# Second channel-mix product by Strassen: seven half-width products per pair of tiles, weight sums on VectorE, and a new placement of the tiles in SBUF

## The chip, the core and the metric

The kernel runs on one NeuronCore of a Trainium2 chip. TensorE does the matrix products and accumulates into PSUM; VectorE (DVE), ScalarE (ACT) and GpSimd (POOL) do the elementwise work; SyncE (SP) and ACT issue the DMAs. Each engine works through its own queue in order and waits on semaphores for the others. The metric is the device time of one execution in microseconds. Before the change it is 2437.73 us, the median of three runs (2437.52 to 2438.23).

## The reference

512 tokens of width 1024 pass through two layers. All inputs, weights and results are float32.

```
for i in range(DEPTH):                       # DEPTH = 2
    h = rmsnorm(x, norm1_g[i]);  z = h @ w_in[i] + b_in[i]
    y_m = mLSTM branch (4 heads, 256 wide)   # scores, decay, values, head norm, output gate
    y_r = retention branch (4 heads, 256 keys, 512 values)
    merged = sigmoid(gm) * (y_m @ w_bm[i]) + sigmoid(gr) * (y_r @ w_br[i])
    x = x + merged @ w_out[i]
    h2 = rmsnorm(x, norm2_g[i])
    x = x + square(relu(h2 @ w_ff1[i] + b_ff1[i])) @ w_ff2[i] + b_ff2[i]     # 1024 -> 4096 -> 1024
    h3 = rmsnorm(x, norm3_g[i])
    x = x + sigmoid(h3 @ w_pe_gate[i]) * (p[i] @ w_pe[i])
return rmsnorm(x, final_g)
```

The change is in the product with `w_ff2`, in the order of the retention gates, and in where tiles lie.

## The kernel before

Activations lie transposed, features on partitions and the 512 tokens on the free axis. A weight tile of 128 rows by 128 columns is the stationary operand and 512 tokens stream past it. For accuracy each float32 operand is kept as two float32r parts, `hi` (a rounded copy that ACT makes) and `lo` (the rest, `src - hi`, that DVE makes). A product is three matmuls, hi by hi, hi by lo and lo by hi (`mm3`, lines 195 to 198).

Weights come as a stream of units of 128 by 1024 floats, 512 KB each, in the order of use. `load_unit` (from line 166) issues the DMA of a unit on SP into one of four raw buffers (`wr`), then has ACT copy it to `wh` (line 183) and DVE subtract to get `wl` (line 185); there are three buffers of each. `unit` keeps two units ready beyond the one in use. `t8` multiplies the 8 activation tiles with one unit: 24 matmuls into one PSUM bank of 8.

The layer runs in program order on TensorE: the projections, the mLSTM heads, the retention heads, the merge (`br_tile`, with the eight sigmoid gates of the retention branch kept on chip in `sB`), the out projection (`wo`), the channel mix, the embedding. The tile framework writes the waits and may move an instruction of another engine ahead of one that is not ready; on the chip the queues then run in the order that it wrote.

The channel mix takes the 4096 hidden columns in four blocks of 1024. For a block, eight `t8` calls make the hidden tiles (`l0f`, `l1f`): DVE multiplies the PSUM tile with the reciprocal root (line 745), ACT adds the bias and takes the relu (746), POOL squares (747), and `split` (210, 211) makes hi and lo. Then eight more `t8` calls multiply the hidden tiles with a unit of `w_ff2` each (`l0fo`, `l1fo`), and DVE adds each result into the residual `x` (777 for the first block, 779 for the others). In the last block each finished tile of `x` goes at once to the operands and squares of the third norm (`Norm.tile`, lines 241, 242, 254, 260). Then come the two `PE` units (the product with `p`), the third norm's `finish` and `spread`, and the gate product `pg`. At the very end four units of weights stay on chip and are used twice, with 256 tokens each time (`pl`).

In SBUF all pools exist for the whole kernel. The value tiles `vh`, `vl` and the temporaries are 516 floats wide, and `mh`, `ml` (the operand of `wo`) use the slots of the query and key tiles for four tiles and those of the value tiles for the other four.

Of the kernel before, what the change touches and what calls it, by code (L numbers as in the profile page):

```python
# [22 lines left out]
P = 128  # L23
# [6 lines left out]
EPS = 1e-6  # L30
UN = 1024
LOOK = 2
LAST = 4

# columns of w_in
# [3 lines left out]
# columns of the per-partition vectors  # L39
# [9 lines left out]

def unit_list():  # L50
    """What each unit of the weight stream holds, in the order of use (one layer)."""
# [48 lines left out]
    full("w_in", CGR)  # L100
# [11 lines left out]
    full("w_br", 0, 1024)  # L112
    full("w_out")
    for b in range(4):
        full("w_ff1", b * 1024)
        full("w_ff2", 0, b * 1024)
    u.append(("PE", 0))
    u.append(("PE", 1))
    full("w_pe_gate")
# [3 lines left out]
def build(ctx, tc, ins, out):  # L123
    nc = tc.nc
    ve, ac, gp, te = nc.vector, nc.scalar, nc.gpsimd, nc.tensor
    units = unit_list()
# [4 lines left out]

    cpool = pool("const", 1)
    wpool = pool("w", 3)
    apool = pool("act", 8)
    bpool = pool("big", 2)
    spool = pool("head", 4)
    tpool = pool("tmp", 7)
    opool = pool("one", 1)
    cols = pool("cols", 2)
    psum = pool("ps", 8, space=bass.MemoryType.PSUM)  # L140

    xs_dram = tc.dram_tile([KT, P, T], F32, name="x_spill")

# [10 lines left out]
    sel = cpool.tile([H, H, P], F32R, name="sel")  # L154
    cos = cpool.tile([P, T], F32, name="cos")
    sin = cpool.tile([P, T], F32, name="sin")
# [4 lines left out]
    def tmp(name, shape=(P, 516)):  # L161
        return tpool.tile(list(shape), F32, name=name, tag="t")

# [1 line left out]
    ready = []  # L165
    nxt = [0]

    def load_unit():
        n = nxt[0]
        if n >= L * NU:  # L170
            return
        nxt[0] += 1
        raw = wpool.tile([P, UN], F32, name=f"wr{n}", tag="wr", bufs=4)
        nc.sync.dma_start(raw, ins["wstream"][n])
        if n >= L * NU - LAST:
            hi = [apool.tile([P, T], F32R, name=f"wh{n}{a}", tag="Ah") for a in range(2)]
            lo = [apool.tile([P, T], F32R, name=f"wl{n}{a}", tag="Al") for a in range(2)]
            for a in range(2):
                split(raw[:, a * T:(a + 1) * T], hi[a], lo[a])
            ready.append((units[n % NU], hi, lo))  # L180
            return
        wh = wpool.tile([P, UN], F32R, name=f"wh{n}", tag="wh")
        ac.activation(wh, raw, AF.Copy)  # L183
        wl = wpool.tile([P, UN], F32R, name=f"wl{n}", tag="wl")
        ve.tensor_sub(wl, raw, wh.bitcast(F32))  # L185
        ready.append((units[n % NU], wh, wl))

    def unit(kind):
        while len(ready) < LOOK + 1 and nxt[0] < L * NU:
            load_unit()  # L190
        u, wh, wl = ready.pop(0)
        assert u[0] == kind, (u, kind)
        return u, wh, wl
# [15 lines left out]
    def split(src, hi_ap, lo_ap):  # L209
        ac.activation(hi_ap, src, AF.Copy)  # L210
        ve.tensor_sub(lo_ap, src, hi_ap.bitcast(F32))

    def acts(side, name):
        hi, lo = [], []
        for k in range(KT):
            hi.append(apool.tile([P, T], F32R, name=f"{name}h{k}", tag=f"{side}h"))
            lo.append(apool.tile([P, T], F32R, name=f"{name}l{k}", tag=f"{side}l"))
        return hi, lo

# [1 line left out]
    class Norm:  # L221
        """Of the token tiles j0 .. j1 - 1."""

        def __init__(self, name, side, i, gain, j0=0, j1=NT):
# [3 lines left out]
            self.act = acts(side, name) if side else None  # L228
# [15 lines left out]
        def square(self, k, x, pool=False):  # L244
            w = self.n * P
            x = x[:, self.s]
            if self.sum is None:
                sq = opool.tile([P, T], F32, name=f"{self.name}sum", tag="bv" if self.s.start else "ssum")[:, :w]
# [26 lines left out]
        def spread(self):  # L275
            n = self.name
            w = self.n * P
            dh = opool.tile([P, 1280], F32R, name=f"{n}dh", tag="ph")[:, :w]
# [198 lines left out]
    for i in range(L):  # L477
# [214 lines left out]
        for c in range(KT):  # L692
            gate_tile(sB, c, "bgr")
# [255 lines left out]
```

## Time and profile before

| | before |
|---|---|
| median of three runs | 2437.73 us |
| profiled execution, first to last instruction | 2435.6 us |
| TensorE matmul busy | 2412.0 us (99%), 11068 records |
| DVE busy | 1349.9 us (55%) |
| ACT busy | 928.9 us (38%) |
| POOL busy | 231.0 us (9%) |
| HBM read | 226.30 MB, 95 GB/s over the span |

The profiled execution gives its span, from its first to its last instruction; the three runs are timed from outside, 2.1 us longer in the median. Matmuls are pipelined: the profile shows each as 0.39 us long for 512 columns, but the next one starts sooner, so the time of a stage is read from start to start or from a window, never from the mean duration. DVE and ACT instructions also start a little before the end of the one ahead of them. In the rows, PE is TensorE's matmuls, PEld its weight loads, and "idle before" is the time in which the engine did nothing just ahead of the instruction, with what ended it.

### The profile page before, as it was taken

How to read it: one execution, taken by the hardware profiler on the slowest of the kernel's cores; microseconds unless marked ns; L12 is line 12 of the kernel's file. 1: busy time of each engine (PE TensorE's matmuls, PEld its weight loads, DVE VectorE, ACT ScalarE, POOL GpSimd, SP SyncE). 2: the span in 40 equal slices, each digit the busy share in tenths (PEclk: the TensorE clock that was granted, in tenths of full speed). 3: DMA queues.
4: the chain of work that ended last, by engine and by line, in shares of the span. 5: the costliest groups of instructions: out<-in, count | busy, mean ns of one | idle time of the engine just before them, and what ended most of it. 6: DMA issues, size and time to landing. Idle time of an engine off the chain costs nothing.

```text
span 2435.6 us, 27773 instructions
## 1 busy us (share of the span) xinstructions
PE 2412.0 (99%) x11068; PEld 2006.5 (82%) x11068; DVE 1349.9 (55%) x1974; ACT 928.9 (38%) x1280; POOL 231.0 (9%) x277
## 2 busy tenths in 40 slices
PE   8999999999999999999999999999999999999997
PEld 6888888888888888888888888888888888888887
DVE  7867534666455434435578665446665554434445
ACT  3756323333233423324547552223323333223343
POOL 4000000000000201102101000000000011101122
PEclk9999999999999999999999999999999999999999
DMA  4222232322223333333322222322322242333331
GB/s 165 91 89 77 87 102 89 95 82 90 92 79 123 102 98 100 97 95 104 126 82 91 89 82 93 101 87 87 96 87 87 81 134 89 100 99 95 95 105 52
DMA packets 69498, 232.30 MB, mean 95 GB/s; under 512 B 7540, under 2 KB 9972, under 8 KB 69368
## 3 DMA queue, kind: packets, MB, share of 16 engines
q1 hardware_dynamic: 64040, 220.95, 29.1%
q10 hardware_dynamic: 5328, 9.57, 1.2%
q8 instruction: 87, 1.43, 0.2%
q14 instruction: 43, 0.35, 0.0%
HBM read 226.30 MB, written 4.19 MB: 95 GB/s over the span
## 4 chain that ended last, share of the span: by engine, by line
PE 98%; DVE 1%; ACT 0%; DVEq 0%; POOL 0%; issue 0%; ACTq 0%
PE l1f L196 2%; PE l1f L198 2%; PE l0f L198 2%; PE l1fo L198 2%; PE l0fo L198 2%; PE l0f L196 2%; PE l0fo L197 2%; PE l0f L197 2%; PE l1fo L197 2%; PE l1fo L196 2%; PE l1f L197 2%; PE l0fo L196 2%; PE l0br L196 1%; PE l1br L196 1%; PE l1br L197 1%; PE l0br L197 1%
## 5 line engine op out<-in xcount | busy, mean ns | idle before, releaser
L183 ACT ACTIVATE wh<-wr 128x1024 fp32r<-128x1024 f32 x402 | 426.4, 1061 | 1105.5 <-issue 210.2
L185 DVE TENSOR_TENSOR wl<-wr,wh 128x1024 fp32r<-128x1024 f32 x402 | 493.3, 1227 | 174.6 <-ACT wh L183 172.6
L196 PE MATMUL l1f<-l1n2h,wh 128*128 128x512 f32 x256 | 99.7, 389 | 0.0
L196 PE MATMUL l0f<-l0n2h,wh 128*128 128x512 f32 x256 | 99.7, 389 | 0.0
L198 PE MATMUL l0f<-l0n2h,wl 128*128 128x512 f32 x256 | 99.6, 389 | 0.0
L198 PE MATMUL l1f<-l1n2h,wl 128*128 128x512 f32 x256 | 99.6, 389 | 0.0
L197 PE MATMUL l0f<-l0n2l,wh 128*128 128x512 f32 x256 | 99.6, 389 | 0.0
L197 PE MATMUL l1f<-l1n2l,wh 128*128 128x512 f32 x256 | 99.6, 389 | 0.0
L747 POOL TENSOR_TENSOR l1ft<-l1ft 128x512 f32<-128x512 f32 x32 | 45.8, 1431 | 255.9 <-ACT l1ft L746 251.8
L747 POOL TENSOR_TENSOR l0ft<-l0ft 128x512 f32<-128x512 f32 x32 | 45.7, 1431 | 255.9 <-ACT l0ft L746 251.8
L197 PEld LDWEIGHTS l0f<-l0n2l,wh 128*128 128x128 f32 x256 | 48.1, 188 | 10.1
L197 PEld LDWEIGHTS l1f<-l1n2l,wh 128*128 128x128 f32 x256 | 48.1, 188 | 10.1
L198 PEld LDWEIGHTS l1f<-l1n2h,wl 128*128 128x128 f32 x256 | 48.1, 188 | 10.0
L198 PEld LDWEIGHTS l0f<-l0n2h,wl 128*128 128x128 f32 x256 | 48.0, 188 | 10.0
L196 PEld LDWEIGHTS l0f<-l0n2h,wh 128*128 128x128 f32 x256 | 48.1, 188 | 9.9
L196 PEld LDWEIGHTS l1f<-l1n2h,wh 128*128 128x128 f32 x256 | 48.1, 188 | 9.9
L779 DVE TENSOR_TENSOR l1x<-l1fo,l1x 128x512 f32<-128x512 f32 x24 | 16.6, 691 | 67.1 <-PE l1fo L198 67.1
L779 DVE TENSOR_TENSOR l0x<-l0fo,l0x 128x512 f32<-128x512 f32 x24 | 16.6, 691 | 66.0 <-PE l0fo L198 66.0
L745 DVE TENSOR_TENSOR l0ft<-l0f,l0n2rb 128x512 f32<-128x512 f32 x32 | 22.0, 691 | 35.7 <-PE l0f L198 35.7
L745 DVE TENSOR_TENSOR l1ft<-l1f,l1n2rb 128x512 f32<-128x512 f32 x32 | 22.0, 691 | 35.6 <-PE l1f L198 35.6
L711 DVE TENSOR_TENSOR l0brt<-l0br,l0sB 128x512 f32<-128x512 f32 x16 | 11.1, 692 | 36.2 <-PE l0br L198 36.2
L711 DVE TENSOR_TENSOR l1brt<-l1br,l1sB 128x512 f32<-128x512 f32 x16 | 11.1, 691 | 36.2 <-PE l1br L198 36.2
(2001 smaller groups left out, 6852.7 us busy)
## 6 DMA issues: line engine op xcount, KB each, us to landing
wr<-wstream SPq DMA_DIRECT2D x406, 512.0 KB, 3.5
x<-xT SPq DMA_DIRECT2D x4, 512.0 KB, 5.9
l0xr<-xT ACTq DMA_DIRECT2D x8, 256.0 KB, 2.5
x_spill<-l0x ACTq DMA_DIRECT2D x8, 256.0 KB, 2.8
l1xr<-x_spill ACTq DMA_DIRECT2D x8, 256.0 KB, 2.6
out<-l1x SPq DMA_DIRECT2D x4, 256.0 KB, 2.6
out<-l1x SPq DMA_DIRECT2D x2, 384.0 KB, 3.9
l0pt<-pT ACTq DMA_DIRECT2D x2, 256.0 KB, 2.7
```

The lines of the kernel that those rows point to most:

```text
L183: ac.activation(wh, raw, AF.Copy)
L185: ve.tensor_sub(wl, raw, wh.bitcast(F32))
L196: te.matmul(o, sh, mh, start=first, stop=False)
L197: te.matmul(o, sh, ml, start=False, stop=False)
L198: te.matmul(o, sl, mh, start=False, stop=last)
L711: ve.tensor_tensor(t[:, :T], o, sB[:, c, :], OP.mult)
L745: ve.tensor_tensor(t[:, :T], o, n2.b, OP.mult)
L747: gp.tensor_tensor(t[:, :T], t[:, :T], t[:, :T], OP.mult)
L779: ve.tensor_tensor(x[:, c, :], o, x[:, c, :], OP.add)
```

## The change

**The second product of the channel mix.** Two output tiles of 128 columns form a pair, and for a block of 1024 hidden rows the pair's product is done by a Strassen scheme (in Winograd's form): the weights are split in four quarters (even or odd hidden tile, first or second output tile), the tokens in two halves of 256, and seven products of half size take the place of eight. One product is 4 tiles times 3 matmuls, 12 matmuls of 256 tokens.

- Weights: a pair takes two units of the stream (the same bytes as before). From them come four pieces: `B11` (a quarter, 512 wide) and `t1`, `t2`, `t3` (1024 wide each, two sums or quarters side by side). DVE makes four sums of 512 columns; each piece is then split into hi (ACT) and lo (DVE).
- Hidden tiles: two neighbouring tiles give eight quarters of 256 columns, four plain and four sums (`pair_operand`); seven of them, hi and lo, are kept.
- Results: the seven products run in three PSUM banks, and four of them (P3, P4, P6, P7) are added on top of what a bank already holds. DVE adds the bank into a 256-token half of `x` after every product: seven adds of 256 columns, and a product that accumulates on a bank must wait until the add before it has read it.
- Order: `pair_schedule` puts P4 of a pair behind P1 of the next one. The first hidden pair of the next block is computed ahead of the four output pairs of a block, and ahead of the last block's output pairs come the two `PE` units.

**The first product** makes two hidden tiles at a time; relu and square are both on ACT, and POOL does neither.

**The retention gates** are computed in the merge loop instead of being kept in `sB`; the first half of the product with `w_br` is written to DRAM and read back, eight tiles of 256 KB each way and layer.

**Placement.** Value tiles are 576 floats wide instead of 516, a 64-byte `pad` comes ahead of the weight buffers, and a tile of 16 or 48 floats (`shift`) moves the tiles of the channel mix. Pools are opened and closed by phases of the layer, on alternate sides of SBUF, with temporaries in the pool of the phase (two of them in the channel mix); `sel`, `cos` and `sin` are loaded once per layer.

**The weight stream** is prepared by pieces (`prep_next`, `ready`); two units instead of one are loaded ahead of `x` at the start.

```diff
+PRODUCTS = {"P1": ("B11", 0, 0), "P2": ("t1", 1, 2), "P3": ("t2", 1, 6), "P4": ("t3", 1, 1), "P5": ("t1", 0, 4),
+            "P6": ("t2", 0, 5), "P7": ("t3", 0, 3)}
+PIECE = ("B11", "t1", "t2", "t3")
+READY = {"P1": 2, "P4": 0, "P5": 3, "P2": 3, "P6": 5, "P3": 5, "P7": 6}
+def pair_schedule(n):
+    out = []
+    for i in range(n):
+        out.append((i, "P1"))
+        if i:
+            out.append((i - 1, "P4"))
+        out += [(i, x) for x in ("P5", "P2", "P6", "P3", "P7")]
+    out.append((n - 1, "P4"))
+    return out
...
+    def prep_next():
...
+        if x in PIECE:
+            r1, r2 = raws[n, 0], raws[n, 1]
+            c0, c1 = slice(0, Q), slice(Q, UN)
+            if x == "B11":
+                src, out_ = r2[:, c0], piece(cur["xw"], "b", Q)
+            elif x == "t1":
+                raws[n, "t"] = t = cur["xw"].tile([P, UN], F32, name=f"t{n}", tag="t")
+                ve.tensor_tensor(t[:, c0], r1[:, c0], r2[:, c1], OP.add)
+                ve.tensor_tensor(r1[:, c0], r1[:, c0], r2[:, c0], OP.add)
+                src, out_ = r1, piece(wpool, "w")
+            elif x == "t2":
+                ve.tensor_tensor(r2[:, c0], r1[:, c0], r2[:, c1], OP.add)
+                src, out_ = r2, piece(wpool, "w")
+            else:
+                src, out_ = raws.pop((n, "t")), piece(cur["xw"], "t")
+                ve.tensor_tensor(src[:, c1], r2[:, c0], r1[:, c1], OP.add)
...
+        split(src, *out_)
...
+        def product(self, x):
+            w, half, j = PRODUCTS[x]
+            ready(place[self.n, "B11"] + READY[x])
+            wh, wl = [a[:, half * Q:(half + 1) * Q] for a in pieces[self.n, w]]
+            b = {"P2": "b", "P5": "c", "P3": "c"}.get(x, "a")
+            first = x in ("P1", "P2", "P5")
+            if first:
+                self.bank[b] = ps(f"{self.name}{b}")
+            o = self.bank[b][:, 0:S]
+            m = slice(j * S, (j + 1) * S)
+            for k in range(4):
...
+                te.matmul(o, wh[:, s], h[:, m], start=f, stop=False, skip_group_check=True)
+                te.matmul(o, wh[:, s], l[:, m], start=False, stop=False, skip_group_check=True)
+                te.matmul(o, wl[:, s], h[:, m], start=False, stop=e, skip_group_check=True)
+            self.done(x, o)
...
+    def pair_operand(name, st, hi, lo):
+        v = st.rearrange("p (q t) -> p q t", t=S)
+        ve.tensor_tensor(v[:, 4:6, :], v[:, 1:3, :], v[:, 0:1, :].to_broadcast([P, 2, S]), OP.subtract)
+        ve.scalar_tensor_tensor(v[:, 6, :], v[:, 5, :], -1.0, v[:, 1, :], OP.mult, OP.subtract)
+        ve.scalar_tensor_tensor(v[:, 7, :], v[:, 6, :], -1.0, v[:, 3, :], OP.mult, OP.subtract)
+        split(st[:, 4 * S:8 * S], hi[:, 3 * S:7 * S], lo[:, 3 * S:7 * S])
+    def pair_quarters(st, hi, lo):
+        split(st[:, S:4 * S], hi[:, 0:3 * S], lo[:, 0:3 * S])
...
-        vh = [spool.tile([P, 516], F32R, name=f"{nm}vh{j}", tag="vh") for j in range(NT)]
+        vh = [cur["low"].tile([P, 576], F32R, name=f"{nm}vh{j}", tag="vh", bufs=NT) for j in range(NT)]
...
-    load_unit()
+    fill_raws(2)
     for k in range(0, KT, 2):
         nc.sync.dma_start(x[:, k:k + 2, :], ins["xT"][k:k + 2].rearrange("k p t -> p k t"))
...
+            o = t8(yr, f"l{i}br0{c}")
+            ac.activation(t[:, :T], o, AF.Copy)
+            nc.scalar.dma_start(br_dram[i, c], t[:, :T])
...
-            br_tile(c, yr)
+            nc.scalar.dma_start(t[:, :T], br_dram[i, c])
+            g = gated(f"l{i}gr{c}", t8(xa, f"l{i}gr{c}"), n1, AF.Sigmoid, bcol(i, "bgr", c))
+            o = t8(yr, f"l{i}br1{c}")
+            ve.tensor_tensor(t[:, :T], o, t[:, :T], OP.add)
+            ve.tensor_tensor(t[:, :T], t[:, :T], g[:, :T], OP.mult)
+            ve.tensor_tensor(mA[:, c, :], mA[:, c, :], t[:, :T], OP.add)
...
-            gp.tensor_tensor(t[:, :T], t[:, :T], t[:, :T], OP.mult)
-            split(t[:, :T], hid[0][c], hid[1][c])
+                ve.tensor_tensor(a, o, n2.b, OP.mult)
+                ac.activation(a, a, AF.Relu, bias=bcol(i, "bf1", 8 * b + 2 * p + d))
+                ac.activation(a, a, AF.Square)
...
+                def done(x_, o):
+                    if x_ in ("P1", "P2"):
+                        add(1, o, OP.add)
+                    elif x_ == "P5":
+                        add(2, o, OP.subtract)
+                    elif x_ in ("P6", "P3"):
+                        add(3, o, OP.subtract)
+                    elif x_ == "P7":
+                        add(2, o, OP.subtract)
+                    elif x_ == "P4":
+                        add(0, o, OP.add)
+                        if b == 3:
+                            for c in (2 * p, 2 * p + 1):
+                                n3.tile(c, x[:, c, :])
```

More of the change, by code (lines that the diff above doesn't have):

```diff
@@ L30 @@
 EPS = 1e-6
+Q = 512
+S = 256
 UN = 1024
 LOOK = 2
+RAWS = 4
+PIECES = 3
+PAD = 16
 LAST = 4
@@ L188, in unit, with tmp, split @@
-    def unit(kind):
-        while len(ready) < LOOK + 1 and nxt[0] < L * NU:
-            load_unit()
-        u, wh, wl = ready.pop(0)
-        assert u[0] == kind, (u, kind)
-        return u, wh, wl
+    def tmp(name, dt=F32):
+        return cur["tmp"].tile([P, T], dt, name=name, tag="t", bufs=cur["ntmp"])
+    def split(src, hi_ap, lo_ap):
+        ac.activation(hi_ap, src, AF.Copy)
+        ve.tensor_sub(lo_ap, src, hi_ap.bitcast(F32))
+    order, loads = [], []
+    for n, u in enumerate(units):
+        if u[0] == "PAIR":
+            order += [(n, x) for x in PIECE]
+            loads += [(n, 0), (n, 1)]
+        else:
+            order.append((n, 0))
+            loads.append((n, 0))
@@ L195, in mm3, with ready @@
+    def ready(k):
+        while at["prep"] < min(len(order), k + 1):
+            prep_next()
+    def unit(kind):
+        n = at["unit"]
+        at["unit"] += 1
+        assert units[n][0] == kind, (units[n], kind)
+        ready(place[n, 0] + LOOK)
+        return units[n], *pieces.pop((n, 0))
     def mm3(o, sh, sl, mh, ml, first, last):
@@ L247, in square @@
             if self.sum is None:
-                sq = opool.tile([P, T], F32, name=f"{self.name}sum", tag="bv" if self.s.start else "ssum")[:, :w]
+                sq = opool.tile([P, T], F32, name=f"{self.name}sum", tag="ssum" + self.half)[:, :w]
             else:
@@ new lines, in ff2, with make, add @@
+        def ff2(b, p):
+            def make(n):
+                nm = f"l{i}o{b}{p}"
+                started = set()
+                def add(q, o, op):
+                    y = x[:, 2 * p + q // 2, (q % 2) * S:(q % 2 + 1) * S]
+                    if b == 0 and q not in started:
+                        started.add(q)
+                        ve.scalar_tensor_tensor(y, y, bcol(i, "bf2", 2 * p + q // 2), o, OP.add, op)
+                    else:
+                        ve.tensor_tensor(y, y, o, op)
+                def done(x_, o):
[12 more added lines that the diff above has]
+                                n3.tile(c, x[:, c, :])
+                return Pair(nm, n, [hid[b, k] for k in range(4)], done)
+            return make
```

357 lines of the change are left out of this document (213 added, 144 removed).

## The prediction

> **What bounds the kernel now.** I read the page's head first, then the shares of the chain of work that ended last, then windows over the stages that the change touches, then single rows of the timeline.
>
> ```profile
> span 2435.6 us, 27773 instructions
> ...
> PE 2412.0 (99%) x11068; PEld 2006.5 (82%) x11068; DVE 1349.9 (55%) x1974; ACT 928.9 (38%) x1280; POOL 231.0 (9%) x277
> ...
> DVE  7867534666455434435578665446665554434445
> ...
> PEclk9999999999999999999999999999999999999999
> ...
> PE 98%; DVE 1%; ACT 0%; DVEq 0%; POOL 0%; issue 0%; ACTq 0%
> ```
>
> TensorE is busy for 99% and 98% of the last chain is matmuls, at full granted clock in every slice. Nothing else can shorten this kernel: a gain has to come out of TensorE's own time. DVE is half idle on average, in the channel mix (slices 14 to 19 and 34 to 39) 30 to 50% busy.
>
> The next rows are windows (window; its length; busy us and instructions of PE, PEld, DVE, ACT and POOL; clock, DMA share, GB/s): the first output stage of the channel mix, the out projection, the whole channel mix of layer 0. Below them, two rows of the timeline (start, duration): the first of 84 matmuls of 256 columns at the kernel's end, and the one that follows the 84th.
>
> ```profile
> 854.80:898.30 43.50, 43.50 (x193) 36.04 (x192) 16.45 (x17) 9.74 (x11) 1.47 (x1) 1.00 0.29 97
> ...
> 764.70:808.90 44.20, 44.20 (x193) 36.04 (x192) 21.19 (x25) 17.06 (x23) 11.38 (x15) 1.00 0.46 144
> ...
> 808.90:1159.40 350.50, 350.50 (x1555) 290.45 (x1554) 154.69 (x179) 118.55 (x147) 56.97 (x42) 1.00 0.31 98
> ```
> ```profile
> 2395.37 0.28 PE L196 MATMUL pl<-l1n3h,wh 128*128 128x256 f32 x1
> ...
> 2405.45 0.28 PE L196 MATMUL pl<-l1n3h,wh 128*128 128x256 f32 x1
> ```
>
> 192 matmuls of 512 tokens take 43.50 us, 0.2266 us each, with no gap; 84 of 256 tokens take 10.08 us, 0.120 us each, with a weight load for each. So a half-width matmul costs 0.53 of a full one: seven half-size products for eight do not save an eighth.
>
> **The change, part by part.** (1) *Matmuls of the second product.* Removed: 2 layers x 4 blocks x 192 matmuls, 8 x 43.50 = 348.0 us. Added: 2 x 16 pairs x 84 matmuls, 32 x 10.08 = 322.6 us. TensorE's floor falls by **25.4 us**. [...]
>
> (2) *Alignment.* In the out projection half of the 192 matmuls read operands from 516-float slots: 44.20 us against 43.50, 0.70 us a layer.
>
> ```profile
> 690.50:697.60 7.10, 7.08 (x30) 5.55 (x30) 1.78 (x3) 1.00 0.26 75
> ```
>
> This is a retention head's product with the values, also from 516-float slots: 30 matmuls in 7.10 us where 30 x 0.2266 is 6.80. Eight heads and two projections give up to 8 x 0.30 + 2 x 0.70 = 3.8 us; some of a head's 0.30 is a wait at its end, so I take **-2.5 us**. The new kernel also shifts the channel mix's operands by 16 or 48 floats. Were that as bad as the 516-float slots (0.70/96 = 7.3 ns a matmul), 2688 matmuls would lose 19.6 us; I take 0, since all the new widths are multiples of 64 floats, like the tiles that run at 0.2266.
>
> (3) *DVE in a pair.* Spacing of DVE instructions from start to start, then durations by group and the 256-column add:
>
> ```profile
> 1504.34 0.68 DVE L599 TENSOR_TENSOR l1r0brku<-l1r0brku,l1r0brkw 128x512 f32<-128x512 f32 x1
> 1504.95 0.74 DVE L598 SCALAR_TENSOR_TENSOR l1r0brkw<-l1r0brkz,bc,cos 128x512 f32<-128x512 f32 x1
> 1505.61 1.21 DVE L185 TENSOR_TENSOR wl<-wr,wh 128x1024 fp32r<-128x1024 f32 x1
> 1506.75 0.68 DVE L211 TENSOR_TENSOR l1r0kl<-l1r0brku,l1r0kh 128x512 fp32r<-128x512 f32 x1
> ```
> ```profile
> L185 DVE TENSOR_TENSOR wl<-wr,wh 128x1024 fp32r<-128x1024 f32 x402 | 493.3, 1227 | 174.6 <-ACT wh L183 172.6
> ...
> L802 DVE TENSOR_TENSOR l1pgt<-pl,l1n3rb 128x256 f32<-128x256 f32 x8 | 3.4, 422 | 4.1 <-PE pl L198 3.9
> ```
>
> In a stream a 512-column operation costs DVE 0.61 us, a 1024-column one 1.14, and a 256-column add some 0.34 (0.42 less the same 0.08 of overlap). A pair needs four sums (2.44), four lo parts (0.61 + 3 x 1.14 = 4.03) and seven adds (2.38): **8.85 us of DVE in 10.08 us of TensorE**, 88%. Two tiles before took 2 x 1.14 + 2 x 0.61 = 3.5 us in 10.9. In the last block two norm operands come on top (2 x 0.66): 10.2 us, over the limit by a little. The hidden pairs need 2 x 0.61 for the root, 0.87 + 1.14 for lo, 0.61 + 2 x 0.40 for the sums and 2 x 1.14 for the weights, 6.9 us in 10.9. So DVE fits, in the output stage barely; what decides is whether it is free at the moments that TensorE needs it.
>
> (4) *The accumulating banks.* P7 lands on the bank that P6 filled, with P3 between them; P4 on the bank of P7, with the next pair's P1 between. How fast the add is done shows at the end of the 256-token products and at the start of the kernel:
>
> ```profile
> 2406.76 0.28 PE L198 MATMUL pl<-l1n3h,wl 128*128 128x256 f32 x1
> 2406.89 0.28 PE L196 MATMUL pl<-l1n3h,wh 128*128 128x256 f32 x1
> ...
> 2407.16 0.42 DVE L802 TENSOR_TENSOR l1pgt<-pl,l1n3rb 128x256 f32<-128x256 f32 x1 [1.16 <-PE pl L198]
> ```
> ```profile
> 11.65 8.05 DVE L242 SCALAR_TENSOR_TENSOR l0n1l<-x,bc,l0n1h 128x512 fp32r<-128x512 f32 x5
> ...
> 19.76 0.50 PE L197 MATMUL l0if<-l0n1l,wh 128*128 128x512 f32 x1 [0.72 <-DVE l0n1l L242]
> ```
>
> The free DVE starts 0.27 us after the next product's slot began (2407.16 - 2406.89), takes 0.42, and TensorE follows 0.06 later (19.76 after 19.70): 0.75 us. A product between them lasts 12 x 0.12 = 1.44, so 0.69 us of slack. In the last pair of a group P4 follows P7 with nothing between: 0.75 us of idle, 4 groups a layer, **+6.0 us** in all; this one nothing can hide. For the other 24 P4 and 32 P7 the bounds are 0 (DVE free) and 0.54 each (the add waits behind a full lo part, 1.23 + 0.75 - 1.44), 0 to 30 us. DVE is inside one of its three long lo parts for a third of the time, and only the first 0.54 us of such a part is harmful: I take 0.1 us each, **+5.6 us**.
>
> (5) *Pieces of weights.* A sum on DVE, the hi copy on ACT and the lo part on DVE are a chain for t1, t2 and t3. `B11` and `t3` have one buffer each, t1 and t2 share three. `t3` can be started when P4 of the pair before has ended (1.44 us of slots after P1) and is needed by P7: 2.88 to 8.64 on the pair's clock, for a chain of about 1.06 + 1.23 + 0.1. t1 of the next pair follows it (sums 1.22, 1.06, 1.23) and is needed at 12.96. Both fit with 3 us to spare if DVE fills ACT's time with other work. In the group's first pair the lo parts of the hidden tiles compete. **+4 us** for the entries of 8 groups and for the third norm's last two tiles (below), between 0 and 13 us: 8 x 1.23 + 2 x 1.6.
>
> (6) *ACT and POOL.* POOL's squares go to ACT:
>
> ```profile
> L183 ACT ACTIVATE wh<-wr 128x1024 fp32r<-128x1024 f32 x402 | 426.4, 1061 | 1105.5 <-issue 210.2
> ...
> L747 POOL TENSOR_TENSOR l0ft<-l0ft 128x512 f32<-128x512 f32 x32 | 45.7, 1431 | 255.9 <-ACT l0ft L746 251.8
> ...
> L241 ACT ACTIVATE l0n3h<-l0x,bc 128x512 fp32r<-128x512 f32 x8 | 5.7, 709 | 0.0
> ```
>
> An output pair gives ACT 3 x 1.06 + 0.63 = 3.8 us of 10.08, a hidden pair under 7 of 10.9: no bound, 0. POOL loses its longest link (1.43 us per tile).
>
> (7) *Moved work.* The two `PE` units go ahead of the last four pairs, with the same 48 matmuls. They covered the third norm's end: now the gate product starts right behind the last P4 and needs tile 6 after 18 x 0.2266 = 4.1 us, for an add, ACT 0.71 and DVE 0.74, some 2.2 us with waits. Covered unless DVE is over 1.6 us behind; that is in (5). The gates of the retention branch move to the merge loop: same matmuls; eight 256 KB writes and reads a layer on ACT's queue; the chain of the last tile grows to three DVE steps, ACT and a lo part, 3 x 0.69 + 0.63 + 0.68, under the 7 x 0.68 = 4.8 us before the out projection needs it: 0. At the layer boundary SP waits for the old pool's tiles before it loads `sel`, with the weight units behind it; four raw buffers and the prepared pieces hold over 20 us of TensorE's work: 0. At the start a second unit of 512 KB goes ahead of `x` (GB/s in 40 slices of the first 25 us):
>
> ```profile
> GB/s 0 0 5 153 111 386 402 397 393 400 410 410 383 390 393 403 413 413 413 341 371 377 413 400 406 413 321 0 0 0 0 0 0 0 0 197 341 282 98 164
> ```
>
> 512 KB at 400 GB/s is 1.3 us, part of it in the slow first slices of the queue: **+1.0 us**, between 0 and 2.
>
> **Sum.** -25.4 - 2.5 + 6.0 + 5.6 + 4.0 + 1.0 = -11.3 us against the profiled 2435.6: 2424.3. The runs' median lies 2.1 us above that span, so **2426 us**, 0.5% faster.
>
> **The rivals.** *All waits but the bare one vanish* (adds always find DVE free, entries and start cost nothing): -25.4 - 2.5 + 6.0, 2416 us. For it: 12% of DVE is free in a pair, and the written order can put the adds first. Against: each lo part is 1.23 us that cannot be interrupted.
>
> *The gain is eaten at the group ends*: each of the 8 last P4 waits for a full lo part of the next stage's weights too, 8 x 1.98 = 15.8 instead of 6.0: 2436 us, no change. For it: just then the queue prepares three units. Against: it would have to hit all eight.
>
> *DVE becomes the bound.* Its waits for ACT between a sum and a lo part stay uncovered: each is 1.06 + 0.14 = 1.2 us, and in the row of line 185 DVE does wait for ACT, 172.6 us over 402 parts. With one of three uncovered a pair takes 8.85 + 1.2 = 10.05, still under 10.08; with two 11.25, 32 x 1.17 = 37.4 us in place of the 5.6: 2458 us; with three 12.45 and 2497 us. It decides from 0.53 us a pair on (the other terms leave 16.9 us over 32 pairs). Against it: in the rows above, DVE went from one kind of work to another with no gap. This is the rival on the other side.
>
> [...]
>
> **How the numbers follow.** A run of this kernel tells 0.2%, 4.9 us, from no change. Forecast 0.45 (own range 2417 to 2433), waits vanish 0.18, gain eaten 0.14, DVE the bound 0.20, no surcharge 0.03. Faster: 0.43 + 0.18 + 0.03 = 0.64; same: 0.02 + 0.12 = 0.14; slower: 0.20 + 0.02 = 0.22. The range reaches from 2410 (the second case with 2 ns less a matmul) to 2458 (two waits uncovered).
>
> **What would show it.** Right: 1344 matmuls of 256 columns a layer at 0.120 us; idle of TensorE ahead of each group's last P4 near 0.75 us and little elsewhere; DVE some 85 to 90% busy in the output pairs; the out projection at 43.5 us. Wrong: a pair at 11 us or more with TensorE waiting for lo parts; half-width matmuls at other than 0.12 us; a stall at the layer boundary or where the gate product starts.

## The result, and the profile after

The changed kernel takes **2442.3 us** (median of 15 runs, 2438.4 to 2447.3), the kernel before 2438.1 (15 runs beside it). The ratio is 1.0021 with a 95% interval of 1.0013 to 1.0029: slower by 0.2%, where 0.5% faster was forecast. All times are medians; one execution of a later version (under "The end") took 6198 us and is left out of its figures. The profiled execution has a span of 2436.7 us. From its page:

```profile
PE 2390.5 (98%) x12220; PEld 2040.2 (84%) x12220; DVE 1574.1 (65%) x2403; ACT 1042.2 (43%) x1420; POOL 142.1 (6%) x213
...
PE 95%; DVE 3%; ACT 1%; issue 1%; POOL 0%; DVEq 0%; ACTq 0%; POOLq 0%
```

TensorE is busy 21.5 us less than before (2390.5 against 2412.0), so the saving is there; but the chain that ended last holds 95% TensorE and 3% DVE where it held 98% and 1%. The waits of TensorE, longest first (us in total, times, longest):

```profile
PE l0if L296 <- ACT l0n1h L390: 8.4, 1, 8.4
PE l1n41ss L417 <- ACT l1n41sq L403: 5.1, 1, 5.1
PE l0pe L296 <- ACT l0pth L231: 4.2, 1, 4.2
PE l1pe L296 <- ACT l1pth L231: 4.2, 1, 4.2
PE l1n40rp L434 <- DVE l1n40dh L431: 2.3, 1, 2.3
PE l0o33a L338 <- DVE l0x L950: 2.0, 1, 2.0
...
PE l0o32a L338 <- DVE l0x L950: 1.9, 1, 1.9
```

The first is the load of `x` at the start, as before (7.2 us there). Layer 1 has the same two waits at `o32` and `o33`. All but the first fall into three places: the `PE` units of each layer (line 296 on `pe`), the last four output pairs of each layer (`o31` to `o33`), and the end of the last layer (`n40`, `n41`). Now the output pairs by windows, layer 0: the four groups of four pairs. The columns are the stretch, then busy time and count of PE, PEld, DVE, ACT and POOL, the granted clock, the DMA share and GB/s.

```profile
861.90:903.30 41.40, 41.40 (x343) 40.84 (x343) 36.39 (x58) 17.45 (x19) 0.00 (x0) 1.00 0.32 107
945.50:986.80 41.30, 41.30 (x344) 40.67 (x344) 35.49 (x58) 17.30 (x19) 0.00 (x0) 1.00 0.32 109
1029.00:1070.10 41.10, 41.05 (x344) 40.60 (x342) 35.50 (x58) 17.23 (x19) 0.00 (x0) 1.00 0.32 109
1119.40:1172.20 52.80, 47.66 (x359) 44.70 (x357) 42.73 (x61) 23.83 (x32) 9.44 (x6) 0.97 0.27 90
```

In the first three groups TensorE all but never stops: 41.4 us for 336 half-width matmuls and 7 or 8 full-width ones that the framework has put in between. Less 7 x 0.2266 = 1.6, a half-width matmul takes 39.8 / 336 = 0.118 us. The fourth group is the one in which the third norm's tiles are made: TensorE is busy for 47.66 of 52.80 us, DVE 42.73, and POOL works beside it, which it does not in the other three. Its clock of 0.97 is the mean of the stretch; behind the wait at `l0o32a` it is lower:

```profile
1150.50:1155.50 5.00, 4.84 (x27) 4.55 (x28) 4.96 (x8) 3.02 (x3) 0.00 (x0) 0.66 0.14 38
```

What happens at the `PE` units, on the timeline of ACT, DVE and TensorE (start, duration; in brackets the idle time and its releaser):

```profile
1101.19 0.39 PE L298 MATMUL l0f<-l0n2h,wl 128*128 128x512 f32 x1
1101.61 0.69 DVE L922 TENSOR_TENSOR l0f33st<-l0f,l0n2rb 128x512 f32<-128x512 f32 x1 [0.64 <-PE l0f L298]
...
1102.92 0.70 ACT L923 ACTIVATE l0f33st<-l0f33st,bc 128x512 f32<-128x512 f32 x1
...
1103.66 0.63 ACT L924 ACTIVATE l0f33st<-l0f33st 128x512 f32<-128x512 f32 x1
1104.32 0.84 ACT L231 ACTIVATE l0hh<-l0f33st 128x768 fp32r<-128x768 f32 x1
...
1105.07 1.13 ACT L231 ACTIVATE l0pth<-l0ptr 128x512 fp32r<-128x512 f32 x2
...
1105.73 1.65 PE L296 MATMUL l0pe<-l0pth,wh 128*128 128x512 f32 x3 [4.16 <-ACT l0pth L231]
```

The hi part of `p` (`l0pth`) is written in the program behind the last hidden pair, so on ACT it stands behind that pair's relu, square and hi part. TensorE has finished the pair at 1101.2 and has nothing else than the `PE` units to go on with. And the idle time has a second price:

```profile
1099.00:1105.70 6.70, 2.58 (x12) 1.80 (x10) 6.01 (x8) 4.86 (x8) 0.00 (x0) 0.89 0.25 84
1105.70:1111.20 5.50, 5.47 (x13) 4.05 (x14) 4.67 (x8) 2.15 (x3) 0.00 (x0) 0.51 0.23 89
1111.20:1119.40 8.20, 8.20 (x38) 6.71 (x37) 1.22 (x1) 4.59 (x8) 0.00 (x0) 1.00 0.21 64
```

For 5.5 us behind the wait at the `PE` units the granted clock is 0.51, and 13 matmuls run where 24 would have. The 48 matmuls that take 11 us at full clock end 18 us after the last hidden one.

### The profile page after: what moved, and what is told of

It reads as the page before. It is cut to its first block, busy times and chain, and to the rows that moved or that the text cites. A ratio compares the mean times of both kernels' runs of the same rounds, so it can differ in the third digit from the quotient of the medians.

```text
span 2436.7 us, 30731 instructions
## 1 busy us (share of the span) xinstructions
PE 2390.5 (98%) x12220; PEld 2040.2 (84%) x12220; DVE 1574.1 (65%) x2403; ACT 1042.2 (43%) x1420; POOL 142.1 (6%) x213
## 4 chain that ended last, share of the span: by engine, by line
PE 95%; DVE 3%; ACT 1%; issue 1%; POOL 0%; DVEq 0%; ACTq 0%; POOLq 0%
PE l0f L296 2%; PE l1f L296 2%; PE l1f L297 2%; PE l0f L297 2%; PE l0f L298 2%; PE l1f L298 2%; PE l1br L297 1%; PE l1br L296 1%; PE l0br L298 1%; PE l0br L297 1%; PE l0br L296 1%; PE l1br L298 1%; PE l1bgm L296 1%; PE l0bgm L296 1%; PE l0wo L297 1%
## 5 line engine op out<-in xcount | busy, mean ns | idle before, releaser
L231 ACT ACTIVATE wh<-wr 128x1024 fp32r<-128x1024 f32 x342 | 361.7, 1059 | 851.8 <-issue 161.4
L232 DVE TENSOR_TENSOR wl<-wr,wh 128x1024 fp32r<-128x1024 f32 x342 | 419.1, 1227 | 216.0 <-ACT wh L231 215.7
L231 ACT ACTIVATE wh_t<-wr 128x1024 fp32r<-128x1024 f32 x64 | 66.9, 1058 | 84.6 <-DVE wr L270 53.6
L232 DVE TENSOR_TENSOR wl_t<-wr,wh_t 128x1024 fp32r<-128x1024 f32 x64 | 77.1, 1218 | 19.4 <-ACT wh_t L231 19.2
L231 ACT ACTIVATE wh_t<-t 128x1024 fp32r<-128x1024 f32 x32 | 33.9, 1061 | 58.6 <-DVE t L277 14.2
L232 DVE TENSOR_TENSOR wl_t<-t,wh_t 128x1024 fp32r<-128x1024 f32 x32 | 39.1, 1222 | 7.6 <-ACT wh_t L231 7.6
L231 ACT ACTIVATE wh_B<-wr 128x512 fp32r<-128x512 f32 x32 | 20.0, 626 | 24.6 <-issue 8.8
L409 POOL TENSOR_TENSOR l0n3sum<-l0n3sum,l0n3sq 128x512 f32<-128x512 f32 x6 | 9.4, 1572 | 348.9 <-issue 319.3
L409 POOL TENSOR_TENSOR l1n3sum<-l1n3sum,l1n3sq 128x512 f32<-128x512 f32 x6 | 8.9, 1487 | 349.3 <-ACT l1n3sum L403 319.7
L297 PE MATMUL l0pg<-l0n3l,wh 128*128 128x512 f32 x64 | 25.0, 393 | 0.2 <-DVE l0n3l L391 0.2
```

Source lines behind the costliest of these rows:

```text
L297: te.matmul(o, sh, ml, start=False, stop=False)
L409: gp.tensor_tensor(self.sum, self.sum, sq, OP.add)
```

## The experiments

The theory: the saving of matmuls is whole, and three things give it back. **A**, `p`'s split stands behind the last hidden pair, and the granted clock is halved behind that wait (0.51). **B**, POOL's sums of the third norm slow DVE in the last group. **C**, the written order of DVE at the end. The main rival, **D**, is the prediction's own: DVE's load in the output pairs. The changed kernel stands at 2442.3, the kernel before at 2437.9 to 2438.1.

### p early

```diff
+            if (kind, b, p) == ("f", 3, 3):
+                pth, ptl = load_p()
             ff1(b, p)
         n2_pool.release()
...
-        pth, ptl = [cur["ff"].tile(...) for a in "hl"]
-        for k in range(2):
-            t = tmp(f"l{i}ptr{k}")
-            nc.scalar.dma_start(t[:, :T], ins["pT"][i, k])
-            split(t[:, :T], pth[:, k, :], ptl[:, k, :])
```

(`load_p` holds the removed lines as they were.)

> The load and split of p are moved ahead of hidden pair (3,3); all else as in the changed kernel. Theory A (the PE units wait for p's hi part, which stands on ACT behind hidden pair (3,3), 4.2 us a layer, and the granted clock is 0.5 for the 6.8 us behind that idle time): the wait at l0pe and l1pe goes, no half clock at 1104 and 2305 us, 7 us a layer, 14 us in all: 2428 us (2425 to 2431). Rival D (DVE cannot keep up with sums, lo parts and adds of the pairs): the work of DVE is the same, the stall only moves into the first pair of the last group: 2439 us or more.

Measured: **2427.0 us** (2426.6 to 2430.3), ratio to before 0.9959 (0.9946 to 0.9971). 15.3 us come back with no work taken away. The tile `l0pth` and the window of the `PE` units:

```profile
L231 ACT ACTIVATE l0pth<-l0ptr x2: 615/616/617, 1094.2 to 1094.8; 128x512 fp32r<-128x512 f32 x2
```
```profile
1101.40:1112.50 11.10, 11.10 (x50) 9.10 (x49) 9.66 (x13) 9.51 (x14) 0.00 (x0) 1.00 0.33 112
```

`p` is split 11 us earlier, the units start right behind the last hidden pair, and run at full clock without a gap. DVE's work is unchanged, so D does not explain these 15 us. The waits in the last group and at the end are still what they were.

### The two PE units behind the last pairs again

```diff
-    u.append(("PE", 0))
-    u.append(("PE", 1))
     pairs(ff_order()[1])
+    u.append(("PE", 0))
+    u.append(("PE", 1))
```

(and the loop over the units behind the call of `run_pairs` for the last group).

> In the changed kernel, the two PE units are put back behind the last four pairs, where they stood before; p's load and split stay in their place. Theory A (it is the moved PE units that wait for p): the 4.2 us waits and the half clock behind them go, and the PE matmuls cover the third norm's end, while the contention in the last four pairs stays: 2426 us (2422 to 2430). Rival (the last hidden pair's late operands stop TensorE whatever follows: the pairs of the last group wait for hidden pair (3,3) in place of the PE units): 2438 us or more.

Measured: **2426.0 us** (2424.7 to 2426.3), ratio 0.9950 (0.9937 to 0.9962). The late split of `p` hurts only because the units were moved ahead of it. The first of the last pairs does wait for the last hidden pair, as the rival has it, but shortly (`PE l0o30a L339 <- DVE l0hl L232` is 0.6 us).

### Matmuls into the idle time

```diff
+        fill = ps(f"l{i}fill")
+        for k in range(16):
+            te.matmul(fill, ones_r, hid[3, k % 2][0][:, 0:T], start=k == 0, stop=k == 15)
         for u in range(2):
             _, wh, wl = unit("PE")
```

> In the changed kernel, 16 full-width matmuls of ready operands into an unused bank (3.6 us) are written ahead of the PE units, into the idle time of 4.2 us. Theory (the half clock follows from TensorE's idle time): the PE units start when they did, but the granted clock stays 1.0 and their matmuls run at 0.227 us, 2.8 to 3.2 us less a layer: 2436.5 us (2434 to 2439). Rival (the half clock has another cause, or the added matmuls delay the units): 2442 us or more.

Measured: **2437.6 us** (2434.7 to 2441.6), 4.7 us less than the changed kernel with 32 matmuls more. The wait is down to what the matmuls do not fill, and the clock stays up:

```profile
PE l0pe L296 <- ACT l0pth L231: 0.5, 1, 0.5
```
```profile
1099.00:1105.70 6.70, 6.70 (x31) 5.53 (x30) 6.02 (x9) 4.90 (x7) 0.00 (x0) 1.00 0.25 80
1107.90:1119.40 11.50, 11.42 (x51) 9.43 (x52) 5.96 (x9) 6.99 (x12) 0.00 (x0) 1.00 0.25 88
```

So cause A has two parts: of its 15.3 us, 7.7 a layer, 4.2 are the wait, and most of the rest is the clock behind it. For this wait of 4.2 us the run shows that the half clock follows from TensorE's idle time: with 16 matmuls without use in it, the clock behind it is 1.00 in place of 0.51, and the kernel is 4.7 us faster. The 0.66 behind the 1.86 us of `l0o32a` has no such run; how the clock stood behind other short waits is in the last section.

### The third norm's sums left out

```diff
-                                n3.tile(c, x[:, c, :])
+                                n3.operand(c, x[:, c, :])
+                                if c in (0, KT - 1):
+                                    n3.square(c, x[:, c, :])
```

> The squares of tiles 1 to 6 of the third norm and POOL's six adds of them are left out (so the third norm's root is of tiles 0 and 7 alone); everything else as in the changed kernel. Theory B (POOL's adds slow DVE's operations that run beside them in the last group): DVE's third norm lo parts fall from 945 ns to about 750, the sums beside them from 1.43 to 0.68, TensorE's waits of 1 to 2 us in the last four pairs go: 5 to 7 us a layer, 2430 us (2426 to 2434). Rival (DVE is over its limit in the last group by its own work, 10.2 us in a pair of 10.1): durations stay, at most 1 us a layer from ACT's six squares: 2440 us or more.

Measured: **2426.9 us** (2426.5 to 2428.4), ratio 0.9955 (0.9942 to 0.9969): 15.4 us. The third norm's lo parts, eight in layer 0 (min/median/max in ns), first in the changed kernel, then without the sums:

```profile
L391 DVE SCALAR_TENSOR_TENSOR l0n3l<-l0x,bc,l0n3h x8: 745/1550/1835, 1133.0 to 1171.4; 128x512 fp32r<-128x512 f32 x8
```
```profile
L391 DVE SCALAR_TENSOR_TENSOR l0n3l<-l0x,bc,l0n3h x8: 744/745/751, 1133.2 to 1165.6; 128x512 fp32r<-128x512 f32 x8
```

The same operation takes up to 1.84 us beside POOL's add and 0.745 without. (The run leaves out ACT's six squares along with the adds; no run takes away one without the other beside the pairs, so it is the rows that point at POOL.) The timeline of the changed kernel shows what is hit (DVE, then POOL):

```profile
1145.90 2.45 DVE L391 SCALAR_TENSOR_TENSOR l0n3l<-l0x,bc,l0n3h 128x512 fp32r<-128x512 f32 x2
1148.27 0.41 DVE L950 TENSOR_TENSOR l0x<-l0x,l0o32b 128x256 f32<-128x256 f32 x1
1148.60 1.43 DVE L269 TENSOR_TENSOR t<-wr,wr 128x512 f32<-128x512 f32 x1
```
```profile
1146.00 3.48 POOL L409 TENSOR_TENSOR l0n3sum<-l0n3sum,l0n3sq 128x512 f32<-128x512 f32 x2 [11.11 <-ACT l0n3sq L403]
```

Of DVE's operations inside POOL's two adds, those with both inputs in SBUF (L391, L269) are longer, L269 by 0.75 us (1.43 against its 0.68 at 1136.0, where POOL does nothing) and the two L391 together by about 1.0; the add of a PSUM bank into `x` (L950) keeps its 0.41. But L950 stands behind them in DVE's order, and TensorE waits for it. In these rows it goes both ways: POOL's two adds are longer too (1.74 each on average, the shortest of the layer's six 1.30). What makes them longer the rows do not show.

### The sums late, on POOL and on DVE

```diff
-                                n3.tile(c, x[:, c, :])
+                                n3.operand(c, x[:, c, :])
...
+        for c in range(KT):
+            n3.square(c, x[:, c, :])
         def pe_evac(o, c, s, nn):
...
             if c == 0:
-                n3.finish()
-                held = o
+                held = []
+            if c < 2:
+                if c == 1:
+                    n3.finish()
+                held.append(o)
                 continue
-            if c == 1:
+            if c == 2:
                 n3.spread()
...
```

> The third norm's squares and POOL's adds come after the last four pairs, beside the gate product, where DVE has little to do; the norm's end is used one tile later (two results of the gate product are held, not one). Theory B: the same gain in the last group as leaving the adds out, 5 to 7 us a layer, less up to 1 us a layer if the norm's root comes late: 2431 us (2427 to 2436). Rival (no contention, only DVE's own load): 2440 us or more.

Measured: **2436.1 us** (2434.1 to 2437.8), 6.2 us less: at the slow edge of the range (its end was 2436), and less than half of what leaving the sums out gives. The waits in the last group are gone, and a new one has come:

```profile
PE l1n3ss L416 <- POOL l1n3sum L409: 2.5, 1, 2.5
...
PE l0n3ss L416 <- POOL l0n3sum L409: 1.7, 1, 1.7
```

Six adds on POOL (1.30 to 1.81 us each in the changed kernel), one behind the other, are not done when the norm's end needs them. With `p` early as well:

> p early and the third norm's sums late together. Theories A and B add up: 14 + 11 us less, 2417 us (2411 to 2424), under the kernel before by 0.6 to 1.1%. Rival (one stall hides the other: what is cleared at the PE units comes back in the last group, since DVE is late by the same amount): 2428 us or more.

Measured: **2424.3 us** (2422.5 to 2424.4), ratio 0.9941 (0.9929 to 0.9954), just outside the range: 18.0 us, not 25. The two waits for POOL's sum are still there (1.7 and 2.6 us), and behind the second of them the clock is halved once more:

```profile
2359.90:2364.60 4.70, 4.70 (x13) 3.64 (x12) 3.79 (x10) 0.00 (x0) 1.79 (x1) 0.50 0.00 0
```

So the adds were given to DVE, which is nearly free beside the gate product: `n3.square(c, x[:, c, :], add=ve)`, where `square` uses `add` in place of `gp`.

> p early; the third norm's squares and adds behind the last four pairs as in the run before, but the adds on DVE, which has little to do there, instead of POOL. Theory: TensorE's waits for POOL's sum (1.7 and 2.6 us) and the half clock behind the second of them (2.2 us) go, and the norm's lo parts of tiles 6 and 7 come in time: 2418 us (2414 to 2422), 4 to 8 us under the version with late adds on POOL. Rival (the order of the last group itself costs the time, POOL has no part in it): 2423 us or more.

Measured: **2414.0 us** (2412.6 to 2414.8), ratio 0.9901 (0.9888 to 0.9915), 13.0 under p early alone, and 10.3 under the late adds on POOL, where 4 to 8 were expected. The adds take 0.69 us each:

```profile
L409 DVE TENSOR_TENSOR l0n3sum<-l0n3sum,l0n3sq x6: 686/692/693, 1156.7 to 1162.1; 128x512 f32<-128x512 f32 x6
```

There is no wait for the sum any more, and the mean granted clock of the profiled execution is 0.997 (0.993 in the changed kernel, 0.998 in the one before).

### The end

In the changed kernel DVE's order at the root of the first half's norm (row of DVE, and of POOL, which makes the root):

```profile
2410.19 0.42 DVE L1018 TENSOR_TENSOR l1pgt<-pl,l1n3rb 128x256 f32<-128x256 f32 x1 [1.97 <-PE pl L298]
2411.10 0.43 DVE L1020 TENSOR_TENSOR l1pgt<-l1pgt,l1pe 128x256 f32<-128x256 f32 x1 [0.48 <-ACT l1pgt L1019]
2411.56 0.42 DVE L1021 TENSOR_TENSOR l1x<-l1x,l1pgt 128x256 f32<-128x256 f32 x1
2411.90 0.48 DVE L431 TENSOR_SCALAR l1n40dh<-ident,l1n40rc 128x128 fp32r<-128x128 f32 x2
...
2418.79 0.42 DVE L1018 TENSOR_TENSOR l1pgt<-pl,l1n3rb 128x256 f32<-128x256 f32 x1 [1.09 <-PE pl L298]
2419.67 3.56 DVE L1052 SCALAR_TENSOR_TENSOR l1x<-l1x,bc,l1n40rb 128x256 f32<-128x256 f32 x5 [0.45 <-ACT l1n40rb L437]
2423.15 0.41 DVE L1020 TENSOR_TENSOR l1pgt<-l1pgt,l1pe 128x256 f32<-128x256 f32 x1
```
```profile
2407.39 0.94 POOL L422 TENSOR_TENSOR l1n40rc<-l1n40ms,nhalf 128x2 f32<-128x2 f32 x1 [3.61 <-DVE l1n40ms L419]
```

The root is there at 2408.33; the diagonal tiles that need it start at 2411.90, since in the order that the framework has written they stand behind the next tile's three steps. And the five final multiplications of the first half, 3.56 us in one piece, stand between the first and the second step of the very last tile. In the kernel before, the framework had written them right behind the root, which is there at 2411.70 (DVE):

```profile
2411.73 0.29 DVE L282 TENSOR_SCALAR l1n40dh<-ident,l1n40rc 128x128 fp32r<-128x128 f32 x1 [0.82 <-POOL l1n40rc L273]
```

TensorE did not wait for them there, and no final multiplication stood between the steps of the very last tile (2420.95 and 2421.91). So this cost is new with the change. The edit makes the diagonal tiles (`diag`, taken out of `spread`) right behind the root, and writes the final multiplications of the first half behind the last tile:

```diff
             if a == 1 and c == KT - LAST:
                 nn[0].finish()
+                nn[0].diag()
             if a == 1 and c == KT - LAST + 1:
                 nn[0].spread()
-                final(nn[0])
+    final(nn[0])
     nn[1].finish()
+    nn[1].diag()
```

> As the run with late adds on DVE, and in the last layer's end the diagonal tiles of the first half's norm are made on DVE right behind its root, and the first half's final multiplications are written behind the last tile. Theory C (the written order of DVE costs the end: 2.5 us of waiting for the diagonal tiles, a half clock behind it, and 3.6 us of final multiplications ahead of the last tile's evacuation): 4 to 6 us less than that run: 2413 us (2409 to 2417). Rival (the end is bound by the chain root, spread, multiplication, output whatever the order): within 1 us of that run.

Measured: **2409.3 us** (2409.1 to 2409.8), ratio to before 0.9883 (0.9868 to 0.9898). The same kernel once more, beside the next one:

> The best version again (p early, the third norm's sums late and on DVE, the end reordered), beside the next run, which differs from it in the second product alone. All theories: 2409.5 us (2408 to 2412), 1.2% under the kernel before.

Measured: **2409.2 us** (2409.1 to 2409.5), ratio to before **0.9882** (0.9869 to 0.9896), 4.8 under the version with the late sums on DVE. Cause C is shown, its two parts only together, and this kernel beats both. A half clock behind the wait for the diagonal tiles, which the expectation names, is not in the changed kernel's profile (1.00 from 2411 to 2416). From the first `pl` matmul to the last instruction the traces have 40.2 us before, 44.9 in the changed kernel and 42.0 here, so 1.8 us of the end's cost are left. In the pairs the longest wait left is 0.8 us. At the end it is this:

```profile
PE l1n41ss L417 <- ACT l1n41sq L403: 3.8, 1, 3.8
```

### The second product undone

In the best version each pair becomes two plain tiles (`t8`) on hidden tiles that are split as a whole; the sums, the banks and the half-width products are gone, everything else stays.

> The best version with the second product undone: each pair is two plain output tiles of 48 full-width slots (24 matmuls of 512 tokens each), without weight sums, quarter sums and half-width products; order, placement, p, norm and end stay. Theory (the matmul saving is real and complete once the stalls are gone: 348.0 us of full-width matmuls against 2688 half-width ones at 0.118, 317.2): 29 to 32 us more, 2440 us (2436 to 2442), so the rest of the change is worth nothing by itself. Rival (DVE's load and the banks still eat part of the saving in the best version): 2425 us or less.

Measured: **2438.7 us** (2438.4 to 2440.5), ratio to before 1.0005 (0.9996 to 1.0014). Strassen alone is worth 2438.7 - 2409.2 = **29.5 us** once nothing stands in its way, all but 1.3 of the 348.0 - 2688 x 0.118 = 30.8 us of matmuls. All the rest of the change together, mended, is worth nothing against the kernel before.

### The weight sums left out

```diff
-                ve.tensor_tensor(t[:, c0], r1[:, c0], r2[:, c1], OP.add)
-                ve.tensor_tensor(r1[:, c0], r1[:, c0], r2[:, c0], OP.add)
...
-                ve.tensor_tensor(r2[:, c0], r1[:, c0], r2[:, c1], OP.add)
...
-                src, out_ = raws.pop((n, "t")), piece(cur["xw"], "t")
-                ve.tensor_tensor(src[:, c1], r2[:, c0], r1[:, c1], OP.add)
+                src, out_ = r2, piece(cur["xw"], "t")
```

> The four weight sums on DVE of every pair are left out (the pieces are split from the raw quarters, so the second product is wrong); all else as in the changed kernel. DVE has 2.4 us less to do in each pair. Theory (DVE has room in the first three groups, and only the last group is too full): the p wait, its half clock and the end stay, the last group's waits shrink by 3 to 6 us a layer: 2433 us (2429 to 2437). Rival D (DVE bounds every group): 30 us or more less, 2412 us or under.

Measured: **2433.8 us** (2432.5 to 2435.4), 8.5 us less. 32 pairs x 2.44 us are 78 us of DVE; taking them away gives 8.5, in the last groups and 0.6 us a layer at the wait for `p`. The first group of layer 0 takes what it took, with 5.2 us of DVE less:

```profile
861.90:903.30 41.40, 41.40 (x342) 40.72 (x341) 31.15 (x48) 17.56 (x19) 0.00 (x0) 1.00 0.35 111
```

DVE is not the bound of the pairs: D falls there. In the last group its load is a condition of B: with the sums gone, and POOL's adds still there, the longest wait of the group falls from 2.0 to 0.9 us.

### The shift tiles left out

The 16- and 48-float tiles are not allocated (`if False:` in `shift`).

> The shift tiles of 16 and 48 floats are left out, everything else as in the changed kernel: the tiles of the channel mix lie 64 or 192 bytes elsewhere. Theory (the place of the tiles matters to a matmul, 1 to 7 ns each, as the 516-float slots did before): 5760 matmuls of the channel mix are slower, 2448 to 2480 us, and the half-width ones go from 118 to 120 ns or more. Rival (the places only have to be multiples of 64 floats, or do not matter): 2442 us.

Measured: **2447.3 us** (2446.1 to 2451.2), ratio 1.0042 (1.0030 to 1.0055), 5.0 us more than with them: between the theory's range and the rival's value. The first three groups again:

```profile
862.20:904.10 41.90, 41.90 (x344) 41.51 (x343) 36.51 (x58) 17.40 (x19) 0.00 (x0) 1.00 0.31 108
946.30:988.10 41.80, 41.80 (x344) 41.40 (x343) 35.61 (x58) 17.21 (x19) 0.00 (x0) 1.00 0.32 108
1030.30:1072.10 41.80, 41.80 (x344) 41.40 (x343) 35.62 (x58) 17.22 (x19) 0.00 (x0) 1.00 0.31 108
```

0.5 to 0.7 us a group, some 1.7 ns for each of its half-width matmuls; eight groups like these would make 4.5 of the 5.0 us. The shift is worth that, and no more: the half-width matmuls run at 0.118 us with it and at 0.120 without.

## Why the prediction failed

The chain of versions splits the difference up (each against the one before it, so that the steps add up by construction): the best version with a plain second product is 0.8 us over the kernel before; Strassen takes 29.5 off; the end as the change has it costs 4.8, the sums beside the pairs 13.0, `p` behind the last hidden pair 15.3. That is 0.8 - 29.5 + 4.8 + 13.0 + 15.3 = +4.4 us, and measured are 2442.3 - 2438.1 = +4.2. The shares depend on the order of the steps; what is left of one stall changes the next.

Against the forecast (2426.4 us before rounding), by these shares: 15.3 for the moved `PE` units, priced at 0; 13.0 for the last groups, priced at 4; 4.8 for the end, not in the sum; the rest at +0.8 in place of -2.5 + 1.0. That makes 15.3 + 9.0 + 4.8 + 2.3 = 31.4 us too slow. Two terms went the other way and hid half of it: the banks, priced at 11.6, cost nothing in the first three groups of a layer (their cost in the last one is part of the 13.0), and the matmuls gave 29.5 in place of 25.4. What is left, 15.7 us, is the distance from forecast to measurement within 0.2.

- **(1) Matmuls, -25.4:** right in kind, too small by 4 to 5 us. The matmuls took 0.118, not the 0.120 of the last product before, because of the placement. The case of no surcharge, given 0.03 among the chances, did not come either: 0.118 is 0.52 of the 0.2266 of a full-width one.
- **(2) Alignment, -2.5:** right. From the last gate product of layer 0 to the channel mix of layer 1 (last `l0pg` to first `l1f`) the traces have 794.0 us before and 792.8 after, 1.2 a layer. The out projection took the forecast time:

```profile
761.60:805.10 43.50, 43.50 (x193) 35.92 (x193) 21.87 (x26) 17.05 (x23) 10.82 (x6) 1.00 0.42 134
```

- The other end of (2), 19.6 us for the shift, was taken as 0; against no shift tiles it gained 5.0.
- **(3) DVE in a pair, 8.85 of 10.08:** right. 35.5 to 36.4 us in four pairs are 8.9 to 9.1 each, and with 86 to 88% TensorE did not wait. The sentence on the last block, "over the limit by a little", is one of the two that failed: it priced the two norm operands at 0.66 us each and did not ask what else runs beside them. They took 1.55 in the median.
- **(4) Banks, +11.6:** far too large. "This one nothing can hide" was wrong: the framework put matmuls of the next hidden pair between P7 and the last P4, six in the first group, and the first three groups lost nothing:

```profile
900.54 0.39 PE L296 MATMUL l0f<-l0n2h,wh 128*128 128x512 f32 x1
...
901.93 0.28 PE L338 MATMUL l0o03a<-l0hh,wh_t 128*128 128x256 f32 x1
```

In the last group the waits do stand on these banks (`o32a` and `o33a` wait for the add in L950), for the reason under (5).

- **(5) Entries and the third norm's last tiles, +4 (0 to 13):** the term that was mis-sized, since the last groups cost 13.0 in all, the top of its range, and for another reason: POOL's adds, not an order of lo parts. The row that said so was in the trace of before, in the longest of the eight lo parts of the third norm, 1872 ns beside a median of 747; there it cost nothing, with DVE free (POOL's add starts 0.03 us behind it, at 1129.09):

```profile
L242 DVE SCALAR_TENSOR_TENSOR l0n3l<-l0x,bc,l0n3h x8: 745/747/1872, 1123.6 to 1161.7; 128x512 fp32r<-128x512 f32 x8
```

- **(6) ACT and POOL, 0:** it counted busy time alone. "POOL loses its longest link" was true, but its other link stayed beside a DVE that had become twice as busy (16.45 of 43.50 us in an output stage before, 36.39 of 41.40 in a group of pairs after).
- **(7) Moved work, 0:** **the step that failed most.** It says of the two `PE` units that they "go ahead of the last four pairs, with the same 48 matmuls", and asks what they had covered behind them; it did not ask what they need. Their operand `p` was ready 38 us before its use in the kernel before (its lo part at 1121.8, the first use at 1159.4), and moving the user ahead by a group of pairs leaves it no time: its split stands behind relu, square and hi part of the last hidden pair on ACT. The runs showed 15.3 us in place of 0: a wait of 4.2 us a layer, and the half clock behind it. In the same term, 4.1 - 2.2 leaves 1.9 us of cover for the third norm's end, not 1.6; nothing came of it, since the gate product waited 0.2 us for its lo part.
- The layer boundary, 0, was right: no wait stands there. The start was forecast at +1.0; the new kernel's trace reaches the channel mix at 805.2 where it was 808.9, and 1.2 of these 3.7 us are (2), so the start gained some 2.5 in that execution.
- The end of the last layer was not in the sum; the late diagonal tiles and the five final multiplications within the last tile cost 4.8 together.

Of the rivals, "the gain is eaten at the group ends" came nearest in time (2436), with the wrong place: not at the eight ends, but within two groups and ahead of them. "DVE the bound" had the right engine for the last groups and the wrong mechanism: not DVE's waits for ACT in every pair, but POOL's adds in one group a layer.

## What to carry to other kernels

When a consumer is moved ahead, look up for each of its operands which instruction makes it and what stands before that on its engine: here 1.1 us of ACT work a layer, written 11 us too late, cost 15 us in two layers. Before DVE is filled to 90%, see what POOL does in the same stretch; an add on POOL that was free beside an idle DVE cost 13 us here, and was cheaper on DVE itself, at another time. And a stall of TensorE can cost more than its length: the waits of 4.2 us here cost 7.7 a layer, most of the rest being the clock behind them.

## What the runs showed that was not expected

- Short waits of TensorE were followed by half a clock in some cases and not in others. In the changed kernel the wait of 1.86 us at `l0o32a` was followed by the 0.66 shown above, and one of 1.87 us at the same place in layer 1 by none (`2351.00:2356.00`, 1.00). With late sums, the same 1.7 us in layer 0 was followed by 2.9 us at 0.50 in one run and by none in another. What parts these cases was not settled; the waits of 4.2 us at the `PE` units had it in both layers of the changed kernel's profile (0.51 in the window above, 0.50 in `2306.00:2311.00`).

```profile
1176.20:1179.10 2.90, 2.90 (x8) 2.27 (x7) 2.35 (x7) 0.00 (x0) 0.52 (x1) 0.50 0.00 0
```
```profile
1164.60:1173.00 8.40, 6.70 (x38) 5.54 (x37) 3.21 (x10) 1.06 (x1) 2.96 (x3) 1.00 0.25 75
```

The first row is the run with late sums on POOL, the second the one with `p` early too.
- With the stalls the runs spread more: the changed kernel's over 8.9 us (15 runs), the mended one's over 0.5 us (4), the one before over 0.8 (15).
